# A two-layer mLSTM and attention trunk on one core: a later start for the third pair of weight buffers, and two products in the other order

## The chip, the core and the metric

The kernel runs on one core of one Trainium2 chip. Its time is device microseconds from launch to end, the median of several runs. The engines that matter are TensorE (PE, with PEld for its weight loads), VectorE (DVE), ScalarE (ACT) and SyncE (SP), which here only issues the transfers between HBM and the on-chip memory. Each engine works through its own instructions in the order in which they were written for it; an instruction that waits holds up all that stand behind it on that engine.

## The reference

The input `x` is 512 tokens of width 2048 in float32. Layer one is an mLSTM with 8 heads, layer two an attention over chunks of 64 with 16 heads. What the change touches are the projections of the first layer, its output product, and the projections of the second layer:

```python
h = modulate(rmsnorm(x, g_pre[l]), shift, scale)
proj = h @ w_in                                   # q, k, v, o, z, gates of layer one
ht = mlstm_chunkwise(q, k, v, li, lf)             # 8 heads
y = sigmoid(o) * rmsnorm(ht, g_head) * silu(z)
x = x + gate * rmsnorm(y @ w_out, g_post[l])      # 4096 -> 2048
kv = hkv @ kv_w                                   # shared keys and values
qz = h @ w_in_b                                   # queries and gate of layer two
```

## The kernel before

**Products in float32.** A float32 matrix is split in two parts, `hi` and `lo`: ACT rounds it (L180, `wh<-wr`), DVE subtracts (L181, `wl<-wr,wh`). Each product of 128 rows is three passes on PE, all issued at L229: hi by hi, hi by lo, lo by hi.

**The stream of weights.** All weights are read as one list of 586 pieces of up to 128x1024, in the order of use; `wpiece` (L186) handles the next one: it loads it (`wr`, L198), splits it into `wh` and `wl`, and gives these to the products. Pieces 0 to 289 are `a_w_in`, 290 to 401 `a_w_out`, 402 to 481 `kv_w`, 482 to 545 `b_w_in`, the rest `b_w_out`. In the order rows below `wh291` is `wh` of piece 291; the number behind it only tells tiles apart.

**Buffers.** Pool `wp` has two buffers for `wr` and two pairs for `wh` and `wl`. While `spare` is set, pieces whose number is a multiple of 3 take their `wr` from a third buffer in another pool; while `spare_w` is set, they take `wh` and `wl` from a third pair there (L214). `spare_w` is unset for heads 3 to 7 of layer one (L671). Behind the last head (h = 7) the pools of that layer are closed (L774 to L776) and a pool `wx` for the third pair is opened (L777). Pools reuse memory: a tile of a new pool waits for the tiles that had the memory before. `wx` lies where temporaries of the heads lay, among them `dd`, which divides the head's output by its norm. The tiles `y` of heads 4 to 7 lie where the gates `zo` of the last head lay, so that they wait until these are written out (`ysc<-zo`, L768).

**The step from the last head to `a_w_out`.** The last head ends in: products `ps_n`, sums of squares through PE (`ps_q`), then on `dd` a multiply-add (L762), a clamp (L763), a square root on ACT (L764), a reciprocal (L765), four products with the gates (L767) and four writes (L768). Then `rows(0, ...)` multiplies the first group of 512 output columns: 16 pieces, 290 to 305, each with 24 products of 512 columns (four row tiles, two blocks of 128, three passes). Its other operand `y` is read back (`yr`, L795 and L800) and split by ACT and DVE (`y<-yr`), two tiles for each piece. In between run sums for the second layer's scale, `adq` (loads L913, sums L900, in a fixed order): five buffers, so a load waits for the sum five before. The next groups of columns (from piece 306) take two row tiles at a time.

**Seven products for eight.** `proj_s` (L274) multiplies two blocks of weight columns by two halves of the tokens with seven products instead of eight, in PSUM banks D, C, A and B. It uses sums of weight blocks, made on DVE (`ws`, L205 to L207) and split into `wsh` and `wsl`, beside the piece itself (`wh`, `wl`); two buffers each. One product is three passes for each of two blocks, with 256 columns. Heads 3 to 7, the keys and the attention's projections go through it.

Which instruction comes where on an engine is set by the scheduler of the programming layer when the program is built: by the order of the code, priorities (weights go ahead of other work) and the buffers that it finds free.

Of the kernel before, what the change touches and what calls it, by code (L numbers as in the profile page):

```python
# [49 lines left out]
def pair_pieces(f, merged=False):  # L50


    sk, nk = list(range(f)), list(range(f, KT // 2))
    n = len(nk)
    assert n <= f
    out = [([[a]], [b]) for a, b in zip(sk, nk)]
    return out + [([sk[i : i + 2]] if merged else [[k] for k in sk[i : i + 2]], []) for i in range(n, f, 2)]
# [75 lines left out]
def hybrid_trunk(ctx, tc, xT, xN, c, adaT, cols, wst, wg, ext, kc, out):  # L133
# [9 lines left out]
    def pool(name, bufs=1, **kw):  # L143
        return tc.tile_pool(name=name, bufs=bufs, reuse_waits="tile", **kw)
# [39 lines left out]
    spare, spare_w = [None], [None]  # L184
# [46 lines left out]
    def mm3(ps, ah, al, bh, bl, start, stop):  # L231
        mm(ps, ah, bh, start, False)
        mm(ps, ah, bl, False, False)
        mm(ps, al, bh, False, stop)
# [15 lines left out]
    def proj_b(mat, xs, pss, ms=range(4), kts=KT, at={}, late=0, summed=0, pl=None):  # L250

        held = []
        for k0 in range(0, kts, 2):
            if k0 in at:
                at[k0]()
            held.append((k0, wpiece(mat, pl=pl, diff=k0 < 2 * summed)))
            if k0 >= kts - 2 * late and k0 < kts - 2:
                continue  # L260
            for group in [[pm] for pm in zip(pss, ms)] if k0 in (0, kts - 2) else [list(zip(pss, ms))]:
                for ka, parts in held:
                    for j in range(2):
                        k = ka + j
                        x = xs(k) if callable(xs) else xs[k]
                        for ps, m in group:
                            t = slice(m * P, (m + 1) * P)
                            other = j == 1 and m > 1 and len(parts) > 1
                            w = slice(0, 512) if other else slice(j * 512, (j + 1) * 512)
                            hi, lo = parts[other]  # L270
                            mm3(ps, x[:, 0, t], x[:, 1, t], hi[:, w], lo[:, w], k == 0, k == kts - 1)
            held.clear()

    def proj_s(mat, xs, ss, f, z1, z2, name, pl, bufs, at={}, merged=False, other=False):  # L274

        D, C, A, B = [(newa if other and n != "d" else newp)(f"ps_{n}{name}") for n in "dcab"]
        pieces = pair_pieces(f, merged)
        begun = set()  # L280
        h0, h1_ = slice(0, 256), slice(256, 512)
        for i, (sk, nk) in enumerate(pieces):
            if i in at:
                at[i]()
            main, *extra = wpiece(mat, [len(ks) for ks in sk], pl, bufs)

            def acc(ps, cols, parts, b, x, last):
                start = id(ps) not in begun
                begun.add(id(ps))
                w = slice(b * P, (b + 1) * P)  # L290
                mm3(ps[:, cols], parts[0][:, w], parts[1][:, w], x[:, 0, :], x[:, 1, :], start, last)

            def eight():
                b0 = 4 * sum(len(ks) for ks in sk)
                for m, k in enumerate(nk):
                    for j in range(2):
                        for t, ps in enumerate((A, B)):
                            acc(ps, slice(0, S), main, b0 + 4 * m + 2 * j + t, xs[2 * k + j], False)

            def seven(g, ks):  # L300
                ns = len(ks)
                b0 = 4 * sum(len(u) for u in sk[:g])
                end = i == len(pieces) - 1 and g == len(sk) - 1
                for ps, cols, t, at_, x, last in (
                    (D, h1_, 0, 1, lambda k: ss[k][1], False),
                    (D, h0, 0, 0, lambda k: xs[2 * k][:, :, h0], end),
                    (C, h0, 1, 1, lambda k: ss[k][2], False),
                    (C, h1_, 1, 0, lambda k: ss[k][0], end),
                    (A, h1_, 1, 2, lambda k: xs[2 * k + 1][:, :, h1_], False),
                    (A, h0, 0, 3, lambda k: xs[2 * k + 1][:, :, h0], end),  # L310
                    (B, h0, 0, 2, lambda k: ss[k][3], end),
                ):
                    if i == 0 and g == 0 and ps is B:
                        eight()
                    for j, k in enumerate(ks):
                        acc(ps, cols, extra[g] if t else main, (0 if t else b0) + at_ * ns + j, x(k), last and j == ns - 1)

            if i:
                eight()
            for g, ks in enumerate(sk):  # L320
                seven(g, ks)
        with tc.high_priority(AHEAD):
            nc.scalar.copy(z1[:, 0, :], D[:, h0])
            nc.vector.tensor_tensor(z2[:, 1, :], z1[:, 0, :], D[:, h1_], op=ALU.add)
            nc.vector.tensor_tensor(z1[:, 1, :], z2[:, 1, :], C[:, h0], op=ALU.add)
            nc.vector.tensor_tensor(z2[:, 0, :], z2[:, 1, :], C[:, h1_], op=ALU.add)
            nc.vector.tensor_tensor(z2[:, 1, :], z1[:, 1, :], C[:, h1_], op=ALU.add)
            nc.vector.tensor_tensor(z1, z1, A.rearrange("p (a t) -> p a t", a=2), op=ALU.add)
            if f < KT // 2:
                nc.vector.tensor_tensor(z2, z2, B.rearrange("p (a t) -> p a t", a=2), op=ALU.add)  # L330
            else:
                nc.vector.tensor_tensor(z2[:, 0, :], z2[:, 0, :], B[:, h0], op=ALU.add)
# [30 lines left out]
    def newp(name):  # L363
        return psP.tile([P, S], F32, tag="p", name=name)
# [409 lines left out]
    hqst.close()  # L774
    hst.close()
    phA.close()  # L776
    spare_w[0] = ctx.enter_context(pool("wx", side="right"))  # L777


    kst = ExitStack()  # L780
# [29 lines left out]
    def gate_row(layer, g, gb=ssum):  # L810

        nc.sync.dma_start(gb, ggd[layer, 4 * g : 4 * g + 4, :].rearrange("k p -> (k p)").partition_broadcast(P))

    def evac(ps, m, g, dst, gated=True, later=None):
        if later is not None:
            later[m] = lambda: nc.vector.tensor_tensor(dst, ps, gb, op=ALU.mult)
        elif gated:
            nc.vector.tensor_tensor(dst, ps, gb, op=ALU.mult)
        else:
            nc.vector.tensor_copy(dst, ps)  # L820
        nc.scalar.activation(newa(f"sqy{m}_{g}"), ps, AF.Square, accum_out=ssq[:, 4 * m + g : 4 * m + g + 1])
# [64 lines left out]
    def rows(g, ms, xs, at={}):  # L886
        ps = [newp(f"ps_y0_{g}_{m}") for m in ms]
        proj_b("a_w_out", xs, ps, ms=ms, kts=32, at=at)
        with tc.high_priority(AHEAD):
            for p, m in zip(ps, ms):  # L890
                yt[m].append(rp.tile([P, S], F32, tag="r", name=f"y{m}_{g}"))
                evac(p, m, g, yt[m][g])
# [4 lines left out]
    def scale_sums():  # L897

        for i, j, a in scale_in:
            pin(nc.vector.tensor_tensor_reduce(  # L900
                a, a, scQ[j], 1.0, mod[:, i : i + 1] if j else col(CB + i), ALU.mult, ALU.add, mod[:, i : i + 1]
            ))
        scale_in.clear()
# [13 lines left out]
    def scale_steps(*ks):  # L917
        at = {k: lambda: (scale_sums(), scale_load()) for k in ks}
        return at | {k + 2: scale_load for k in ks}

    gate_row(0, 0)
    rows(0, range(4), y_tile, scale_steps(4, 10, 16, 22, 28))
    for pair, ms in enumerate(PAIRS):
        for g in range(1, 4):
            at = scale_steps(4, 12, 20, *([28] if g < 3 else [])) if pair == 0 else {}
            if pair == 0 and g == 3:
                at[28] = lambda: (scale_sums(), amul_cols(2, 48 + KT, GPRE + KT))
            if pair == 1 and g == 1:
                at = {2: lambda: residual(0), 4: lambda: residual(1)}
                at |= {20 + 4 * i: lambda i=i: turned(0, [i], False) for i in range(3)}  # L930
            if pair == 1 and g == 2:
                at = {2: lambda: turned(0, [3], False)}
            if pair == 1 and g == 3:
                at = {k: lambda k=k: [key_input(i, kept(i, slice(0, 2 * P)), slice(0, 2 * P)) for i in range(k // 2 - 1, k // 2 + 1)] for k in range(2, 32, 4)}
            gate_row(0, g)
            rows(g, ms, ys, at)
# [352 lines left out]
```

## Time and profile before

| | before |
|---|---|
| median of 3 runs | 2808.89 us (2805.28 to 2811.35) |
| the profiled execution's own time | 2808.36 us |
| its span, first to last instruction | 2806.6 us |
| granted TensorE clock, mean | 0.995 |
| PE, DVE, ACT busy | 98%, 79%, 50% of the span |
| chain that ended last, by engine | PE 88%, DVE 5%, DMA 4%, ACT 2% |
| moved by DMA | 527.12 MB, mean 188 GB/s |

PE is the engine that sets the time. The span is 1.8 us less than the execution's own time: what lies before the first and behind the last instruction. Two kinds of rows carry the argument: windows, which give for a stretch of time the busy time of each engine and the granted clock, and timelines, which list an engine's instructions with the idle time before each and what ended it.

### The profile page before, as it was taken

How to read it: one execution, taken by the hardware profiler on the slowest of the kernel's cores; microseconds unless marked ns; L12 is line 12 of the kernel's file. 1: busy time of each engine (PE TensorE's matmuls, PEld its weight loads, DVE VectorE, ACT ScalarE, POOL GpSimd, SP SyncE). 2: the span in 40 equal slices, each digit the busy share in tenths (PEclk: the TensorE clock that was granted, in tenths of full speed). 3: DMA queues.
4: the chain of work that ended last, by engine and by line, in shares of the span. 5: the costliest groups of instructions: out<-in, count | busy, mean ns of one | idle time of the engine just before them, and what ended most of it. 6: DMA issues, size and time to landing. Idle time of an engine off the chain costs nothing.

```text
span 2806.6 us, 42903 instructions
## 1 busy us (share of the span) xinstructions
PE 2761.2 (98%) x16400; PEld 2455.8 (88%) x16400; DVE 2220.3 (79%) x3664; ACT 1408.2 (50%) x2023; POOL 0.2 (0%) x4
## 2 busy tenths in 40 slices
PE   7999999999999999999997999999999999999998
PEld 5887888888999999989997888888998899999887
DVE  7986979768997887978877467567986798898676
ACT  4234524334555555555556234568534566666523
POOL 0000000000000000000000000000000000000000
PEclk9999999999999999999998999999999999999999
DMA  8975787865332333323337599788535544444686
GB/s 297 311 248 178 231 317 254 290 220 171 100 113 91 99 115 102 114 91 106 113 98 236 173 295 300 253 265 289 176 131 179 168 128 122 129 121 124 218 309 238
DMA packets 185016, 527.12 MB, mean 188 GB/s; under 512 B 19893, under 2 KB 38357, under 8 KB 184169
## 3 DMA queue, kind: packets, MB, share of 16 engines
q1 hardware_dynamic: 184810, 524.38, 56.6%
q8 instruction: 128, 2.10, 0.3%
q14 instruction: 78, 0.64, 0.1%
HBM read 490.69 MB, written 38.85 MB: 189 GB/s over the span
## 4 chain that ended last, share of the span: by engine, by line
PE 88%; DVE 5%; DMA 4%; ACT 2%; issue 1%; SPq 0%; DVEq 0%; ACTq 0%
PE ps_y L229 16%; PE ps_v L229 12%; PE ps_azo L229 4%; PE ps_o L229 4%; PE ps_kv L229 4%; PE ps_czo L229 4%; PE ps_dzo L229 4%; PE ps_qk L229 3%; PE ps_z L229 3%; PE ps_l L229 3%; PE ps_az L229 3%; PE ps_cz L229 3%; PE ps_dz L229 3%; PE ps_bzo L229 2%; PE ps_s L229 2%; PE ps_lead L229 2%
## 5 line engine op out<-in xcount | busy, mean ns | idle before, releaser
L180 ACT CAST wh<-wr 128x1024 fp32r<-128x1024 f32 (+3 forms) x586 | 585.7, 1001 | 751.2 <-PE ps_y L229 220.4
L181 DVE TENSOR_TENSOR wl<-wr,wh 128x1024 fp32r<-128x1024 f32 (+3 forms) x586 | 678.4, 1159 | 257.7 <-ACT wh L180 255.6
L229 PE MATMUL ps_y<-wh,y 128*128 128x512 f32 x1536 | 478.5, 392 | 9.2 <-ACT wh L180 9.2
L229 PEld LDWEIGHTS ps_y<-wh,y 128*128 128x128 f32 x1536 | 289.3, 189 | 69.5 <-ACT wh L180 9.6
L180 ACT CAST wsh<-ws 128x768 fp32r<-128x768 f32 (+2 forms) x240 | 188.8, 787 | 309.5 <-DVE ws L207 102.0
L229 PE MATMUL ps_y<-wl,y 128*128 128x512 f32 x768 | 300.2, 391 | 5.1 <-DVE wl L181 5.1
L229 PE MATMUL ps_v<-wh,h 128*128 128x512 f32 x896 | 285.5, 390 | 0.0
L181 DVE TENSOR_TENSOR wsl<-ws,wsh 128x768 fp32r<-128x768 f32 (+2 forms) x240 | 215.1, 898 | 87.0 <-ACT wsh L180 85.2
L229 PEld LDWEIGHTS ps_v<-wh,h 128*128 128x128 f32 x896 | 168.2, 188 | 34.5
L229 PEld LDWEIGHTS ps_y<-wl,y 128*128 128x128 f32 x768 | 144.9, 189 | 35.5 <-DVE wl L181 5.8
L229 PE MATMUL ps_v<-wl,h 128*128 128x512 f32 x448 | 174.7, 390 | 0.0
L205 DVE TENSOR_TENSOR ws<-wr 128x512 f32<-128x512 f32 (+1 forms) x208 | 139.4, 671 | 31.4 <-DMA wr<-in_wst 29.9
L229 PE MATMUL ps_kv<-wh,hkv 128*128 128x512 f32 x512 | 159.6, 390 | 0.0
L396 DVE CUSTOM_DVE_ANT_0 ada<-ada,scB,mod 128x1024 f32<-128x1024 f32 x96 | 123.0, 1282 | 17.3 <-DMA ada<-in_adaT 16.0
L396 DVE CUSTOM_DVE_ANT_0 ada<-ada,scB,cl 128x1024 f32<-128x1024 f32 x96 | 122.8, 1281 | 16.6 <-DMA ada<-in_adaT 16.5
L229 PEld LDWEIGHTS ps_kv<-wh,hkv 128*128 128x128 f32 x512 | 96.1, 188 | 20.3 <-ACT wh L180 0.4
L229 PE MATMUL ps_kv<-wl,hkv 128*128 128x512 f32 x256 | 100.0, 391 | 1.2 <-DVE wl L181 1.2
L229 PE MATMUL ps_l<-h,wh 128*128 128x512 f32 x320 | 99.2, 392 | 0.6 <-ACT q L489 0.4
L229 PEld LDWEIGHTS ps_v<-wl,h 128*128 128x128 f32 x448 | 84.2, 188 | 17.2 <-issue 0.9
L207 DVE TENSOR_TENSOR ws<-wr 128x256 f32<-128x256 f32 (+1 forms) x208 | 85.7, 413 | 2.7
L206 DVE TENSOR_TENSOR wr<-ws,wr 128x256 f32<-128x256 f32 (+1 forms) x208 | 85.5, 411 | 1.8
L229 PE MATMUL ps_qk<-h,wh 128*128 128x512 f32 x256 | 79.4, 390 | 0.0
(402 smaller groups left out, 6502.9 us busy)
## 6 DMA issues: line engine op xcount, KB each, us to landing
wr<-in_wst SPq DMA_DIRECT2D x520, 512.0 KB, 4.0
ada<-in_adaT SPq DMA_DIRECT2D x224, 512.0 KB, 6.0
adq<-in_adaT SPq DMA_DIRECT2D x64, 256.0 KB, 5.8
xt<-nsc SPq DMA_DIRECT2D x48, 256.0 KB, 4.2
wr<-in_wst SPq DMA_DIRECT2D x30, 256.0 KB, 4.5
yr<-ysc SPq DMA_DIRECT2D x28, 256.0 KB, 6.2
wr<-in_wst SPq DMA_DIRECT2D x16, 384.0 KB, 6.0
bsc<-in_ext SPq DMA_DIRECT2D x16, 320.0 KB, 6.1
```

Of the source, the lines that this page charges most:

```text
L180: nc.scalar.copy(hi, src)
L181: nc.vector.tensor_tensor(lo, src, hi.bitcast(F32), op=ALU.subtract)
L205: nc.vector.tensor_tensor(t[:, : 2 * w], r[:, w : 3 * w], r[:, : 2 * w], op=ALU.subtract)
L206: nc.vector.tensor_tensor(r[:, w : 2 * w], t[:, w : 2 * w], r[:, :w], op=ALU.add)
L207: nc.vector.tensor_tensor(t[:, 2 * w :], r[:, 3 * w :], r[:, w : 2 * w], op=ALU.subtract)
L229: nc.tensor.matmul(ps, a, b, start=start, stop=stop)
L396: pin(nc.vector.tensor_tensor_reduce(at, at, (sc or scB)[:, j * D // 2 : (j + 1) * D // 2], 1.0, mod[:, i : i + 1] if j else col(CB + i), ...
```

## The change

Two edits. `spare_w` is set to `wx` not where the pool is opened but behind the first group of output columns: pieces 290 to 305 all take the two pairs of `wp`, and piece 306 is the first in the third pair. The pool's place in memory stays. And in `proj_s` the last two products into bank A change places: the one with `wh` (block 3, tokens 0 to 255) comes first, the one with `wsh` (block 2, tokens 256 to 511) second.

```diff
-                    (A, h1_, 1, 2, lambda k: xs[2 * k + 1][:, :, h1_], False),
-                    (A, h0, 0, 3, lambda k: xs[2 * k + 1][:, :, h0], end),
+                    (A, h0, 0, 3, lambda k: xs[2 * k + 1][:, :, h0], False),
+                    (A, h1_, 1, 2, lambda k: xs[2 * k + 1][:, :, h1_], end),
                     (B, h0, 0, 2, lambda k: ss[k][3], end),
...
-    spare_w[0] = ctx.enter_context(pool("wx", side="right"))
+    wx = ctx.enter_context(pool("wx", side="right"))
...
     rows(0, range(4), y_tile, scale_steps(4, 10, 16, 22, 28))
+    spare_w[0] = wx
     for pair, ms in enumerate(PAIRS):
```

On ACT, in the last head, while its products `ps_n` are evacuated (`sqs`, `sq`):

```order
 L755 ACTIVATE sqs7_14172<-ps_n7_0_14173 128x512
 L755 ACTIVATE sq7_1_14197<-ps_n7_1_14186 128x512
-L180 CAST wh292_14355<-wr292_14353 128x1024
+L180 CAST wh291_14311<-wr291_14309 128x1024
 L755 ACTIVATE sq7_2_14212<-ps_n7_2_14201 128x512
```

Before, piece 292 was cast here, ahead of 291; now it is 291.

On DVE, where the last head's `dd` is finished (L762 to L765) and applied to the gates (L767):

```order
+L181 TENSOR_TENSOR wl293_14400<-wr293_14397,wh293_14399 128x1024
 L762 SCALAR_TENSOR_TENSOR dd7_14168<-ps_q7_14231,dd7_14168 128x512
-L756 SCALAR_TENSOR_TENSOR zo7_3_0_13922<-ps_n7_3_14216,cl_99,zo7_3_0_13922 128x512
 L763 TENSOR_SCALAR dd7_14168<-dd7_14168 128x512
 L765 RECIPROCAL dd7_14168<-dd7_14168 128x512
+L181 TENSOR_TENSOR wl294_14440<-wr294_14437,wh294_14439 128x1024
 L767 TENSOR_TENSOR zo7_0_0_13202<-zo7_0_0_13202,dd7_14168 128x512
 L767 TENSOR_TENSOR zo7_1_0_13442<-zo7_1_0_13442,dd7_14168 128x512
 L767 TENSOR_TENSOR zo7_2_0_13682<-zo7_2_0_13682,dd7_14168 128x512
 L767 TENSOR_TENSOR zo7_3_0_13922<-zo7_3_0_13922,dd7_14168 128x512
-L181 TENSOR_TENSOR wl291_14312<-wr291_14309,wh291_14311 128x1024
+L181 TENSOR_TENSOR wl295_14488<-wr295_14485,wh295_14487 128x1024
```

The difference of 291 stood behind all of it; now those of 293 and 294 stand in it, and 295 behind.

On DVE further on, among the `adq` sums (each an `ISA` row on its tile and one that reads out the sum):

```order
 L900 ISA adq73_0_14615,mod_102<-adq73_0_14615,scQ0_14347,cl_99 128x512
 L900 ISA mod_102 128x1
+L181 TENSOR_TENSOR wl300_14704<-wr300_14701,wh300_14703 128x1024
 L900 ISA adq74_0_14657,mod_102<-adq74_0_14657,scQ0_14347,cl_99 128x512
 L900 ISA mod_102 128x1
-L181 TENSOR_TENSOR wl297_14572<-wr297_14569,wh297_14571 128x1024
```

At this point of the sums DVE made piece 297 before and makes piece 300 now. Five sums stand ahead of each of 299, 300 and 301 in the changed order, as they stood ahead of 296, 297 and 298.

## The prediction

> **What bounds the kernel now.** I read the page's busy shares first, to see whether any engine is full.
>
> ```profile
> span 2806.6 us, 42903 instructions
> PE 2761.2 (98%) x16400; PEld 2455.8 (88%) x16400; DVE 2220.3 (79%) x3664; ACT 1408.2 (50%) x2023; POOL 0.2 (0%) x4
> ```
>
> TensorE is busy for all but 45.4 us of the span. An edit that changes no product can win only what lies in those 45.4 us, or what makes a product slower than it could be. So the next view is the busy time by stage.
>
> ```profile
> 835.00:1497.00 662.00, 660.41 (x4709) 625.72 (x4708) 547.88 (x850) 366.79 (x468) 0.00 (x0) 1.00 0.32 104
> 1497.00:1550.00 53.00, 38.63 (x168) 31.37 (x168) 43.61 (x67) 31.34 (x49) 0.00 (x0) 0.84 0.87 289
> 1550.00:1608.00 58.00, 58.00 (x257) 48.03 (x256) 21.39 (x33) 11.86 (x12) 0.00 (x0) 1.00 0.49 163
> 2245.00:2630.00 385.00, 382.94 (x3006) 371.96 (x3005) 340.42 (x746) 255.20 (x437) 0.00 (x0) 1.00 0.44 134
> ```
>
> Columns: stretch, its length, busy time of PE, PEld, DVE, ACT, POOL, granted clock, DMA share, GB/s. The long stages (heads 4 to 7, attention) lose 1.6 and 2.1 us. The 53 us around 1520 lose 14.4 us, and there the clock is 0.84. This is the step from the first layer's last head to its output product. The list of waits, cut to that place, names what PE waits for:
>
> ```profile
> PE ps_y L229 <- ACT wh L180: 9.2, 1, 9.2
> PE ps_y L229 <- DVE wl L181: 5.1, 1, 5.1
> ```
>
> Two waits, once each. The timelines of PE, ACT and DVE (start, length, what ran, idle before it) say which weights those are.
>
> ```profile
> 1504.45 0.48 PE L229 MATMUL ps_y<-wh,y 128*128 128x512 f32 x1
> ...
> 1509.99 0.91 PE L229 MATMUL ps_q<-sp_q,ones_r 128*128 128x512 f32 x2
> 1520.14 1.22 PE L229 MATMUL ps_y<-wh,y 128*128 128x512 f32 x2 [9.25 <-ACT wh L180]
> 1526.46 0.79 PE L229 MATMUL ps_y<-wl,y 128*128 128x512 f32 x1 [5.09 <-DVE wl L181]
> ```
> ```profile
> 1501.96 1.05 ACT L180 CAST wh<-wr 128x1024 fp32r<-128x1024 f32 x1
> ...
> 1511.09 1.04 ACT L180 CAST wh<-wr 128x1024 fp32r<-128x1024 f32 x1
> ...
> 1518.53 0.63 ACT L764 ACTIVATE dd<-dd 128x512 f32<-128x512 f32 x1 [1.78 <-DVE dd L763]
> 1519.07 1.03 ACT L180 CAST wh<-wr 128x1024 fp32r<-128x1024 f32 x1
> ```
> ```profile
> 1504.83 1.22 DVE L181 TENSOR_TENSOR wl<-wr,wh 128x1024 fp32r<-128x1024 f32 x1
> ...
> 1519.19 3.35 DVE L765 RECIPROCAL dd<-dd 128x512 f32<-128x512 f32 x1 [0.69 <-ACT dd L764]
> 1522.58 2.50 DVE L767 TENSOR_TENSOR zo<-zo,dd 128x512 f32<-128x512 f32 x4
> 1525.18 1.23 DVE L181 TENSOR_TENSOR wl<-wr,wh 128x1024 fp32r<-128x1024 f32 x1
> ```
>
> By the order of before, the casts at 1501.96 and 1511.09 are pieces 292 and 293, and the one at 1519.07 is 291, which PE needs first. 291 is a multiple of 3, so it takes the third pair, whose memory held tiles of the head that is just ending: its cast stands behind the square root of `dd` (L764), its difference behind the reciprocal and the last products (L765, L767). PE uses 290 at 1504.45 and then has nothing until both are through.
>
> **What the change removes.** PE is idle from 1510.90 (1509.99 + 0.91) to 1526.46, except for two products, which at full pace take 0.45: 15.1 us. What follows is slow as well:
>
> ```profile
> 1526.46 241.51 PE ps_y L229 x1054
> ...
> 1790.60 84.36 PE ps_y L229 x372
> ```
>
> In the chain of work a product takes 84.36/372 = 0.2268 us later on, but the 1054 from 1526.46 take 241.51 instead of 239.0: 2.5 us more. The granted clock (second last but one column) explains it:
>
> ```profile
> 1515.00:1520.00 5.00, 0.00 (x0) 0.00 (x0) 4.30 (x8) 3.20 (x4) 0.00 (x0) 0.50 0.82 234
> ...
> 1535.00:1540.00 5.00, 5.00 (x23) 4.13 (x22) 5.00 (x9) 5.00 (x10) 0.00 (x0) 1.00 0.88 280
> ```
>
> The clock is halved in the idle time and full again by 1535. So 15.1 + 2.5 = **17.6 us** go if PE never waits here. The Trainium skill (TensorE: Matmul & The Clock Gate, Part 1: The HAM clock gate) puts both the idle time that halves the clock and the busy time that restores it at about 3.4 us. By that page each restart costs an estimated 1.7 us, two of them 3.4, and 18.5 would go in place of 17.6; the trace shows half clock but the smaller loss, and I keep the row.
>
> Does PE really not wait? In the changed order 291 stands where 292 stood on ACT and DVE (cast 1501.96, difference done by 1506.05), in the buffers of 289, long left by PE. Its load is one of the pair issued here:
>
> ```profile
> 1495.84 1.17 SPq L198 DMA_DIRECT2D wr<-in_wst  x2
> ...
> 1523.37 2.35 SPq L768 DMA_DIRECT2D ysc<-zo  x4
> ```
>
> It needs to be ready when 290 ends, at 1504.45 + 24 x 0.2268 = 1509.9: four us to spare. A piece lasts 5.44 us; with the 0.45 of `ps_q`, now inside 292, PE reaches 293 at 1521.2, 294 at 1526.7, 299 at 1553.9, 300 at 1559.3 and 301 at 1564.7. 292 and 293 stand in the places of 293 and behind the last early `y` split, done by 1513.9 and 1518.8. 294 is behind the reciprocal: `ps_q` runs some nine products into 292, at 1517.4; behind the difference of 293 (1518.8) come two short steps on `dd` and the square root, together about 1.7, and the reciprocal, 3.35, to about 1523.9, and the difference of 294 (1.22) ends at 1525.1, with 1.8 us to spare.
>
> **What it adds.** Sixteen pieces run on two pairs. A cast can start only when PE leaves the piece two before, 5.44 us ahead of need; cast and difference take 2.3 of it. The rest is cover for whatever DVE's order puts ahead of the difference. Two things stand there. First the `y` splits of heads 4 to 7, which wait for the last `ysc` write:
>
> ```profile
> 1531.89 5.31 ACT L180 CAST y<-yr 128x512 fp32r<-128x512 f32 x10 [11.80 <-DMA ysc<-zo]
> ...
> 1532.55 6.11 DVE L181 TENSOR_TENSOR y<-yr,y 128x512 fp32r<-128x512 f32 x10 [6.14 <-ACT y L180]
> ```
>
> Before, they began 6.2 us after the last write's issue (1523.37 + 2.35). Now this write stands on SP behind the load of 298, which waits for the difference of 295 (1529.0), so it leaves at 1529.5 and the splits begin at 1533.5 to 1535.7. Sixteen splits of 0.61, the differences of 297 and 298, and five `adq` sums of 0.82 bring the difference of 299 to an end at 1552 to 1553.9; needed 1554.1. Second, the `adq` sums, five of them ahead of each of 299, 300 and 301:
>
> ```profile
> 1548.68 1.22 DVE L181 TENSOR_TENSOR wl<-wr,wh 128x1024 fp32r<-128x1024 f32 x1
> 1550.27 0.75 DVE L900 CUSTOM_DVE_ANT_0 adq<-adq,scQ,cl 128x512 f32<-128x512 f32 x1 [0.37 <-DMA adq<-in_adaT]
> 1550.95 0.08 DVE L900 DVE_READ_ACCUMULATOR2_ANT mod<- 128x1 f32 x1
> ...
> 1554.61 1.22 DVE L181 TENSOR_TENSOR wl<-wr,wh 128x1024 fp32r<-128x1024 f32 x1
> ...
> ...
> 1560.66 1.22 DVE L181 TENSOR_TENSOR wl<-wr,wh 128x1024 fp32r<-128x1024 f32 x1
> ```
> ```profile
> 1545.91 3.21 SPq L913 DMA_DIRECT2D adq<-in_adaT  x5
> ```
> ```profile
> adq<-in_adaT SPq DMA_DIRECT2D x64, 256.0 KB, 5.8
> ```
>
> Before, such a round took 5.9 to 6.0 us, because the sums wait for their loads; PE takes 5.44. The third pair hid that. Now 300 ends at 1558 to 1560 (needed 1559.5). 301 adds the load of `adq78`, queued on SP behind the load of 303, which waits for 300: 0.5 + 4.4 to land + 0.82 + 1.22, so 1565 to 1567 against 1564.9. The 4.4 is what the first of the five above took, issued at 1545.91 behind a weight load and summed on landing at 1550.27; the page's median for such loads is 5.8, but this one follows a pause of SP. I take **1.0 us** of new waiting; ends: 0, and 3.5 with every landing at 5.8. Behind 301 only one sum stands before 302, and from 306 the third pair is in use, as before.
>
> The swap of two products moves the last reader of `wsh` by six products, 0.72 us later, in every seven-product piece. It adds no instruction. Cost between a gain of 1.6 (all idle time of heads 4 to 7) and the price in the third rival; nearest is the row of that stage, which hardly waits, so 0.
>
> **Sum.** The profiled execution took 2808.36 us, 0.5 under the median of the runs: 2808.4 - 17.6 + 1.0 = **2791.8**.
>
> **Rivals.**
> 1. The wait comes back on two buffers: landings above 5.8 us in a stage at 0.87 of DMA put 299 to 301, or 294 behind the reciprocal, several us late: 3.5 to 10 us back, 2795 to 2802. For it: the DVE rounds are longer than PE's piece. Against: only three rounds. The same page of the Trainium skill would add a halved clock to any single wait above about 3.4 us; the 9.25 above shows it, no wait that I expect is so long.
> 2. The wait doesn't go: something else holds PE at 1510 as long, or a load lands 10 us later: 2803 to 2814. Against: the order puts 291 in front.
> 3. Slower: the later release of `wsh` reaches PE.
>
> ```profile
> ACT wsh L180 <- PE ps_az L229: 92.8, 46, 2.7
> ...
> L205 DVE TENSOR_TENSOR ws<-wr 128x512 f32<-128x512 f32 (+1 forms) x208 | 139.4, 671 | 31.4 <-DMA wr<-in_wst 29.9
> ```
> ```profile
> 884.29 1.44 PE ps_czo L229 x12
> ```
> ```profile
> 1483.97 1.22 DVE L181 TENSOR_TENSOR wl<-wr,wh 128x1024 fp32r<-128x1024 f32 x1
> ...
> 1486.76 0.40 PE L229 MATMUL ps_dzo<-h1s,wh 128*128 128x256 f32 x2
> ```
>
> ACT does wait for these releases, 46 times in the attention alone, and 208 pieces have them; the six products are half of the 1.44 us of twelve. If PE paid 0.72 each time it were 150 us; from 0.08 us a piece (16.6/208) the gain is gone, and 0.12 gives 2817. Against: the difference of 288 ends at 1485.2 and PE, which began 288 at 1486.76, had 1.6 us in hand, twice the shift.
>
> **How the numbers follow.** Forecast (2788 to 2795) 0.71; rival 1 0.14; rival 2 0.06; rival 3 0.05; better still, with the idle time of other stages gone too, 0.04. A measurement of this kernel tells about 0.2% (5.6 us) from no change; faster by more than that: 0.71 + 0.14 + 0.04 = 0.89, within 0.06, slower 0.05. The range 2787.5 to 2798 holds the forecast and half of rival 1, about 0.8; its ends also take in the spread of the runs, 3 us either way.
>
> **What would show it.** Right: no PE wait above 1 us between 1500 and 1550, a granted clock of 1.00 there, the casts in the order 290, 291, 292; PE some 17 us ahead by 1555, with one or two waits under 2 us on `wl` near 1560 to 1567. Wrong: a PE wait above 3 us at 1510 to 1570, or PE idle in heads 4 to 7 or the attention above the 1.6 and 2.1 us of before.

## The result, and the profile after

The changed kernel takes 2788.69 us in the median of four runs (2784.57 to 2793.66), beside 2810.12 for the kernel before in the same comparison: ratio 0.9928, interval 0.9907 to 0.9948. The execution that was profiled took 2784.57, where before took 2808.36: 23.8 us less. The prediction was 2791.8, 16.6 less. The page's head, and the four stages whose rows were shown of before (the attention's begins 17 us earlier; the other three have the same bounds as before):

```profile
span 2782.7 us, 42823 instructions
...
PE 2751.1 (99%) x16400; PEld 2452.1 (88%) x16400; DVE 2217.3 (80%) x3664; ACT 1401.9 (50%) x2025; POOL 0.2 (0%) x4
```
```profile
835.00:1497.00 662.00, 661.31 (x4718) 626.67 (x4717) 548.79 (x853) 369.58 (x473) 0.00 (x0) 1.00 0.32 104
1497.00:1550.00 53.00, 53.00 (x247) 44.41 (x246) 42.70 (x60) 34.58 (x52) 0.00 (x0) 1.00 0.89 295
1550.00:1608.00 58.00, 56.47 (x250) 46.33 (x249) 33.65 (x62) 16.67 (x22) 0.00 (x0) 1.00 0.70 225
2228.00:2613.00 385.00, 384.34 (x3032) 376.32 (x3031) 342.81 (x753) 252.65 (x443) 0.00 (x0) 1.00 0.45 140
```

The 53 us around 1520, where PE was busy for 38.63 at a clock of 0.84, are full now, at 1.00. A new hole of 1.5 us stands in the next window. PE's busy time in total fell by 10.1 us though the products are the same 16400: part of what went was never idle time.

To see where, I take the time between the first products of two pieces of the weight list, from the timelines of PE. The columns are the stages in the order of the list.

| pieces | work | before, us | after, us | difference |
|---|---|---|---|---|
| 0–149 | before and in heads 0 to 3 | 693.89 | 695.43 | +1.54 |
| 150–289 | the end of head 3, and heads 4 to 7 | 780.68 | 778.91 | -1.77 |
| 290–299 | first output columns | 72.95 | 55.11 | **-17.84** |
| 300–305 | the same, end | 32.64 | 34.51 | **+1.87** |
| 306–401 | other output columns | 264.76 | 264.76 | 0.00 |
| 402–481 | keys and values | 342.87 | 341.39 | -1.48 |
| 482–545 | attention | 396.09 | 390.33 | **-5.76** |
| 546–584 | last product | 178.92 | 178.70 | -0.22 |

Where the text below gives a time for heads 4 to 7, it is that of pieces 150 to 289. Three terms are bold; the other rows together are -1.9, and the experiments show how far such rows move by themselves. The first term is the one that the change was predicted to remove. On ACT and DVE the cast and the difference of 291 now come here (start, length, what ran, idle before):

```profile
1502.70 1.05 ACT L180 CAST wh<-wr 128x1024 fp32r<-128x1024 f32 x1 [1.05 <-DMA wr<-in_wst]
...
1511.24 1.05 ACT L180 CAST wh<-wr 128x1024 fp32r<-128x1024 f32 x1
...
1515.29 1.05 ACT L180 CAST wh<-wr 128x1024 fp32r<-128x1024 f32 x1
```
```profile
1505.55 1.22 DVE L181 TENSOR_TENSOR wl<-wr,wh 128x1024 fp32r<-128x1024 f32 x1
...
1520.73 3.35 DVE L765 RECIPROCAL dd<-dd 128x512 f32<-128x512 f32 x1 [0.70 <-ACT dd L764]
1524.00 1.16 DVE L181 TENSOR_TENSOR wl<-wr,wh 128x1024 fp32r<-128x1024 f32 x1
```

By the order, the casts are 291, 292 and 293; 291 is whole at 1506.8, 2.7 us ahead of PE, which finishes 290 at 1509.5. The difference of 294 is the one behind the reciprocal, done at 1525.2.

The second term is the new wait. The list of waits of PE on weights in this stage has one row (total, times, longest); PE, DVE and SP show it:

```profile
PE ps_y L229 <- DVE wl L181: 1.5, 1, 1.5
```
```profile
1566.57 0.50 PE L229 MATMUL ps_y<-wl,y 128*128 128x512 f32 x1 [1.53 <-DVE wl L181]
```
```profile
1564.62 0.75 DVE L900 CUSTOM_DVE_ANT_0 adq<-adq,scQ,cl 128x512 f32<-128x512 f32 x1 [2.04 <-DMA adq<-in_adaT]
...
1565.30 1.22 DVE L181 TENSOR_TENSOR wl<-wr,wh 128x1024 fp32r<-128x1024 f32 x1
```
```profile
1559.28 0.33 SPq L198 DMA_DIRECT2D wr<-in_wst  x1
1559.66 1.25 SPq L913 DMA_DIRECT2D adq<-in_adaT  x2
```

Piece 301's difference stands behind a sum whose load leaves SP at 1559.66, behind the weights of 303, and lands at 1564.6.

The third term was not predicted. These are windows cut exactly at the attention's first and last piece, of before and of after:

```profile
2217.67:2613.76 396.09, 394.91 (x3157) 386.92 (x3156) 351.01 (x752) 257.70 (x431) 0.00 (x0) 1.00 0.43 131
```
```profile
2199.83:2590.16 390.33, 390.33 (x3157) 386.46 (x3156) 348.77 (x752) 251.28 (x431) 0.00 (x0) 1.00 0.43 133
```

The same 3157 products, the same clock; PE is idle for 1.2 us before and not at all after. The other 4.6 us are in "busy" time. In the rows below a product of 256 columns is listed with 0.28 us, whether the next one starts 0.12 or 0.28 us behind it: a hold shorter than that leaves no gap on PE, and shows only in the weight loads. These are the waits of PEld in that window of before (after has none), then the last block of a head's transposes in before, as the weight load and with the products around it, and such a block in after:

```profile
PEld ps_t L1092 <- DVE pt L181: 2.3, 12, 0.2
PEld ps_t L1092 <- DVE s L1083: 2.0, 4, 0.8
```
```profile
2417.59 0.14 PEld L1092 LDWEIGHTS ps_t<-kcs,s 128*128 128x128 f32 x1 [0.20 <-DVE pt L181]
```
```profile
2416.87 0.38 PE L1092 MATMUL ps_t<-kcs,s 128*128 128x128 f32 x2
2417.00 0.48 PE L229 MATMUL ps_dz<-h2s,wh 128*128 128x256 f32 x2
2417.32 0.28 PE L229 MATMUL ps_dz<-h2s,wl 128*128 128x256 f32 x1
2417.60 0.33 PE L1092 MATMUL ps_t<-kcs,s 128*128 128x128 f32 x1
```
```profile
2421.39 0.38 PE L1093 MATMUL ps_t<-kcs,s 128*128 128x128 f32 x2
2421.53 0.48 PE L229 MATMUL ps_dz<-h2s,wh 128*128 128x256 f32 x2
...
2422.56 0.28 PE L229 MATMUL ps_dz<-h,wl 128*128 128x256 f32 x1
2422.68 0.28 PE L1093 MATMUL ps_t<-kcs,s 128*128 128x128 f32 x1
```

In the attention each head's scores `s` are transposed block by block on PE (`ps_t`), and ACT and DVE split the result (`pt`). Before, the last block stands three products behind the block ahead of it, and DVE has not yet read the bank that it takes: the product in front takes 0.28 from start to start where it takes 0.12 otherwise. After, it stands nine products behind and waits for nothing. Over the 71 places where a product is followed by a transpose, the mean start to start is 177 ns before and 120 after. Added up over the stage, the steps to a transpose took 4.0 us less after, those between transposes 1.1 and those behind them 0.8; all other steps from one start to the next add up to the same within 0.1 us. So the whole gain lies at the transposes, and the other products are as fast in either order.

### The profile page after: what moved, and what is told of

It reads as the page before. It is cut to its first block, busy times and chain, and to the rows that moved or that the text cites. A ratio compares the mean times of both kernels' runs of the same rounds, so it can differ in the third digit from the quotient of the medians.

```text
span 2782.7 us, 42823 instructions
## 1 busy us (share of the span) xinstructions
PE 2751.1 (99%) x16400; PEld 2452.1 (88%) x16400; DVE 2217.3 (80%) x3664; ACT 1401.9 (50%) x2025; POOL 0.2 (0%) x4
## 4 chain that ended last, share of the span: by engine, by line
PE 84%; DVE 6%; DMA 5%; issue 2%; ACT 2%; SPq 0%; DVEq 0%; ACTq 0%
PE ps_y L229 14%; PE ps_v L229 12%; PE ps_kv L229 5%; PE ps_o L229 4%; PE ps_azo L229 4%; PE ps_czo L229 4%; PE ps_dzo L229 4%; PE ps_az L229 3%; PE ps_cz L229 3%; PE ps_dz L229 3%; PE ps_qk L229 3%; PE ps_z L229 3%; DMA ada<-in_adaT 2%; PE ps_bzo L229 2%; PE ps_s L229 2%; PE ps_n L229 2%
```

## Experiments

Each kernel ran beside the kernel before on the same chip, five rounds. Diffs are against the changed kernel.

**The changed kernel again.**

> The changed kernel again, beside the others. Theory: as before minus 21 us; waits at 301 alone, 1.5 us. A rival that takes the attention's gain for chance of one execution: its heads would then last 25.1 us or more here.

2789.85 us (2785.78 to 2790.6), ratio 0.9928 [0.9915, 0.994]. Attention 390.32 and pieces 290 to 299 in 55.00, as in the first profile. But pieces 300 to 305 took 36.37, 3.7 more than before, though the wait was hardly longer:

```profile
PE ps_y L229 <- DVE wl L181: 1.8, 1, 1.8
```
```profile
1565.00:1570.00 5.00, 3.17 (x11) 2.54 (x11) 3.59 (x6) 0.86 (x1) 0.00 (x0) 0.83 0.78 267
1570.00:1575.00 5.00, 5.00 (x20) 4.07 (x19) 0.00 (x0) 1.01 (x1) 0.00 (x0) 0.82 0.51 167
```

The clock (third column from the end) falls behind this wait: the row from 1570 to 1575 has 20 products, where that of the first profile has 24 at a clock of 1.00. That is the other half of the 3.7 us.

**One edit at a time.** First, the third pair late, the two products in the old order:

```diff
-                    (A, h0, 0, 3, lambda k: xs[2 * k + 1][:, :, h0], False),
-                    (A, h1_, 1, 2, lambda k: xs[2 * k + 1][:, :, h1_], end),
+                    (A, h1_, 1, 2, lambda k: xs[2 * k + 1][:, :, h1_], False),
+                    (A, h0, 0, 3, lambda k: xs[2 * k + 1][:, :, h0], end),
```

> Third pair from piece 306 on, bank A in the order of before. Theory: the wait at the step to the output product goes in full (17.9 us from piece 290 to 300), one wait of 1.5 to 2 us at piece 301 comes, and the attention stays as it was before (each head 25.1 to 25.4 us), since its order on PE is that of before: about 16 us below before. Rival: the 5.8 us that the changed kernel gained in the attention come from the earlier arrival of that stage, not from the order of bank A; then this run gains them as well, about 22 us.

2795.59 us (2794.11 to 2798.71), ratio 0.9953 [0.994, 0.9967]: 13.3 less than before. Pieces 290 to 299 in 55.00, 300 to 305 in 35.75 (two waits, 2.5 us together), attention 395.75.

Second, the new order of the two products, the third pair early:

```diff
-    wx = ctx.enter_context(pool("wx", side="right"))
+    spare_w[0] = ctx.enter_context(pool("wx", side="right"))
...
-    spare_w[0] = wx
```

> Bank A in the new order alone, third pair from piece 290 as before. Theory: both waits at piece 291 stay (9.2 and 5.1 us, clock 0.50 behind them), and the attention gains 0.28 us a head, 5 to 6 us in all, because its order on PE is that of the changed kernel: 4 to 6 us below before. Rival: the new order is worth nothing, and the time is that of before within 1 us; second rival: the later release of the sums costs PE something in heads 4 to 7, and the time is above before.

2804.71 us (2802.45 to 2809.04), ratio 0.9983 [0.9974, 0.9992]: 4.2 less. Its list of waits has the old pair of rows unchanged, and its attention takes 390.35:

```profile
PE ps_y L229 <- ACT wh L180: 9.2, 1, 9.2
...
PE ps_y L229 <- DVE wl L181: 5.1, 1, 5.1
```

So each edit has its own place: the late third pair removes the wait at 291 and nothing in the attention, the swap the reverse. 13.3 and 4.2 make 17.5, where both together gave 19.1 on this chip.

**The third pair early, but not for the two pieces that meet the head's tail.** The new order of the products, and:

```diff
-            pw = spare_w[0] if spare_w[0] and i % 3 == 0 else wp
+            pw = spare_w[0] if spare_w[0] and i % 3 == 0 and i not in (291, 294) else wp
...
+    spare_w[0] = ctx.enter_context(pool("wx", side="right"))
...
-    spare_w[0] = wx
```

> Bank A in the new order, third pair from piece 290 on but not for 291 and 294, so that it begins with 297. Theory: no wait at 291, since nothing of the last head is waited for; the third pair also takes the five sums one piece further ahead, so that the wait of 1.5 us at 301 goes: 1.5 to 2 us below the changed kernel, PE without a wait from 1497 to 1608. Rival: the wait at 301 is one of DMA for the weights themselves, and stays.

2787.22 us (2785.25 to 2791.06), ratio 0.9922 [0.9909, 0.9935]. No wait of `ps_y` at all: 55.01 for 290 to 299 and 32.64 for 300 to 305. With the third pair in use from 297 the wait at 301 is gone, so that wait is a price of two pairs. Its whole time isn't told apart from that of the changed kernel; heads 4 to 7 took 782.10 in its profile, 3.2 more than in the changed kernel, with the same order on VectorE and ScalarE up to there.

**The third pair early, but not for 291 alone** (as above with `i not in (291,)`), so that 294 is the first in it.

> New order of the two products; the third pair opened where it was before, but piece 291 alone takes the two common pairs. 294 takes the third, and its cast and difference now stand behind those of 296. Theory 1 (the old wait was the place of the third pair's cast and difference behind the tail of the head, for whichever piece first takes it): PE waits for wh and wl of 294 at about 1526, 2.1 and 1.4 us by the order and the durations of before, so pieces 290 to 300 take 57.5 to 59 in place of 55.1, no wait at 301 (300 to 306: 32.64). Theory 2 (it was 291's place alone): no wait at 294, 290 to 300 in 55.0, whole time as with 291 and 294 both left out, about 2787. If the clock falls after such short waits, 1 to 2 us more.

2788.64 us (2784.16 to 2793.77), ratio 0.993 [0.9918, 0.9942]. Pieces 290 to 299 took 57.97, and PE waits at 294:

```profile
1530.61 1.21 PE L229 MATMUL ps_y<-wh,y 128*128 128x512 f32 x4 [2.12 <-ACT wh L180]
...
1532.06 0.50 PE L229 MATMUL ps_y<-wl,y 128*128 128x512 f32 x1 [0.24 <-DVE wl L181]
```

Theory 1 holds: the wait goes with the third pair, to whichever piece is first in it; 2.1 on the cast as expected, 0.24 where 1.4 was expected on the difference. Here the clock stayed at 1.00.

**The sums moved out of the first group** (two steps of them there in place of five; the rest later):

```diff
-    rows(0, range(4), y_tile, scale_steps(4, 10, 16, 22, 28))
+    rows(0, range(4), y_tile, scale_steps(22, 28))
...
-            at = scale_steps(4, 12, 20, *([28] if g < 3 else [])) if pair == 0 else {}
+            at = scale_steps(4, 10, 16, 22, *([28] if g < 3 else [])) if pair == 0 else {}
```

> The changed kernel, with the 64 sums of the scale moved: two steps of them in place of five in the first group of output columns, more in the later groups. The same work in another order. Theory 1 (the wait of 1.5 to 1.8 us at piece 301 is the rounds of sums ahead of the differences of 299 to 301): no wait there, pieces 300 to 306 in 32.64 in place of 34.5 to 36.4, whole time about 2787.5. Theory 2 (the wait comes from the two pairs alone, or from the load of the weights): the wait stays, 34.5 or more.

2786.82 us (2783.06 to 2792.34), ratio 0.9926 [0.9914, 0.9938]. Pieces 300 to 305 in 32.64, no wait on weights there, 306 to 401 in 264.76 as ever. The wait at 301 needs both: two pairs, and the rounds of sums ahead of the differences.

**The swap in the attention alone, and everywhere but there** (third pair late in both). In the first the old order is kept for all but the attention's `z`; the second reverses the condition:

```diff
+                if name[0] == "z" and name[1].isdigit():
+                    (p5, c5, t5, a5, x5, _), (p6, c6, t6, a6, x6, _) = seq[4:6]
+                    seq[4:6] = [(p6, c6, t6, a6, x6, False), (p5, c5, t5, a5, x5, end)]
```

> Third pair late as in the changed kernel; the two products of bank A in the new order in the attention's projections alone (head, key and z products elsewhere in the old order). Theory 1 (the swap works in the attention alone, because there a product of the old order stands in front of a transpose and holds PE): attention, pieces 482 to 546, 390.3 us as in the changed kernel, whole time about 2790. Theory 2 (the swap works through the heads, and the 5.7 us seen in the attention were that execution's): attention about 396, whole time about 2795 as with the old order everywhere.

> Third pair late; the new order of the two products everywhere but in the attention's projections. Theory 1 (the swap works in the attention alone): attention 395.8 to 396.1 us, whole time about 2795. Theory 2 (it works through the heads): attention 390.3 whatever its own order, or the loss of time elsewhere; whole time about 2790.

In the attention alone: 2785.85 us (2784.58 to 2788.53), ratio 0.9917 [0.9904, 0.993], attention 390.37. Everywhere else: 2792.02 (2788.42 to 2800.5), ratio 0.9944 [0.9931, 0.9957], attention 395.41. Theory 1 holds. Elsewhere the order of the two products shows nothing: heads 4 to 7 took 780.6 us with the old and 779.6 with the new, the keys and values 341.1 and 341.2. The first of the two also had a wait of 2.4 us at 301, and behind it the clock fell:

```profile
1570.00:1575.00 5.00, 5.00 (x17) 3.96 (x16) 0.87 (x1) 0.00 (x0) 0.00 (x0) 0.66 0.89 284
```

**Is it the transposes' place?** The swap does three things in the attention: two products change places; most transposes move 6 to 8 products back; and some work on DVE and ACT is re-ordered. The next kernels keep the old order of the products (as in the first single edit) and move the transposes by their priority:

```diff
+                with tc.high_priority(-40):
+                    nc.tensor.transpose(ps[:, P * (i - j) : P * (i - j + 1)], pr[i][:, P * j : P * (j + 1)], ident)
```

> Third pair late, the two products of bank A in the old order everywhere; in the attention the transposes of the scores have a lower priority, so that most of them stand 9 to 12 products later on PE and those of the last two blocks 36 to 40 later (the changed kernel has most of them 6 to 8 later). The same products in the same order among themselves. Theory 1 (the order of the products itself costs nothing; what the changed kernel gains in the attention is that the transposes come after their scores and banks are ready): attention 390.3 to 391 us, no product ahead of a transpose above 130 ns in the mean, whole time about 2790. Theory 2 (the old order of the products costs the time, by where the sums of weight blocks come): attention 395.5 as with the old order, whole time about 2795.

2793.35 us (2790.99 to 2800.31), ratio 0.9948 [0.9936, 0.9961]; attention 397.40, more than either order. A miss, for a reason that its waits in the attention show:

```profile
PEld ps_o L229 <- DVE pt L181: 3.6, 8, 1.0
PEld ps_t L1094 <- DVE s L1084: 1.2, 2, 0.8
```

The products that read the transposes (`ps_o`) now wait for them, which they never did before. And the hold ahead of the transposes is not gone: 173 ns from start to start in the mean, over 58 places, and the wait for `s` is much as with the old order's own places (1.5 there). Later isn't better by itself. The same priority in the changed kernel, together with the moved sums:

> The changed kernel with the sums of the scale moved out of the first group and the transposes of the attention at lower priority. Theory 1: no wait at piece 301 (300 to 306: 32.64) and attention 389 to 390.3, since the 1 us that PE still waits at the last transpose of a head goes; whole time 2785 to 2788. Theory 2: the late transposes hold up the products that read them, attention above 390.3.

2792.77 us (2787.84 to 2797.89), ratio 0.9943 [0.993, 0.9955]; attention 393.41, 3.1 more than with the changed kernel's places. Pieces 300 to 305 took 32.64, so the sums' part held; the transposes' part didn't, and the time expected was missed.

Last, priorities for each block, chosen so that every transpose stands within one product of its place in the changed kernel (those behind the last head's products excepted), with the old order of the products:

```diff
+                with tc.high_priority(-{(0, 1): 36, (1, 1): 36, (0, 2): 40, (0, 3): 39, (1, 2): 40, (1, 3): 39, (3, 3): 11}.get((j, i), 0)):
+                    nc.tensor.transpose(ps[:, P * (i - j) : P * (i - j + 1)], pr[i][:, P * j : P * (j + 1)], ident)
```

> Third pair late, the two products of bank A in the old order everywhere; in the attention the transposes stand, to within one product, at the places that the changed kernel has (6 to 8 products later than the old order puts them; only behind the last head's products they differ). VectorE and ScalarE keep nearly the order of the old products. Theory 1 (it is the transposes' place on PE): attention 390.3 to 391 us, products ahead of a transpose 120 ns in the mean, whole time about 2790. Theory 2 (it is the order of the other work on VectorE and ScalarE, which makes scores and banks late): the products ahead of a transpose stay near 170 ns, attention 394 to 396, whole time about 2795. Between the two: both have a share.

2791.91 us (2789.03 to 2794.67), ratio 0.9933 [0.992, 0.9947]. Its attention and the waits of PEld in it:

```profile
2201.04:2592.92 391.88, 391.49 (x3158) 386.71 (x3156) 352.84 (x752) 257.88 (x431) 0.00 (x0) 1.00 0.44 132
```
```profile
PEld ps_t L1094 <- DVE pt L181: 1.0, 3, 0.5
```

Of the 5.4 us between 395.75 and 390.33, moving the transposes brings 3.9, with the products in the old order. The attention lies between the ranges of the two theories, and so does the time ahead of a transpose: 146 ns in the mean, over 85 places (14 more, since a single product now stands between two transposes once in each of 14 heads). Both have a share. DVE's order is nearer to the old one than to the changed kernel's, but ACT's differs from both, so the 3.9 are the transposes' places together with what moves around them.

The row of waits for `s` is gone, that for the banks is smaller (2.5 in 13 waits in the run with the old places). Its three waits stand before the last block of three heads, at 2300, 2350 and 2450, nine products behind the block ahead, as in the changed kernel: the place is the same there, but DVE has not yet read the bank. So about 1.0 of the remaining 1.5 comes from when DVE does its work, and not from the place; the rest wasn't told apart.

## Why the prediction was right, and where it was not

**The removed wait: right.** 17.6 was predicted for the idle time and the half clock, 17.84 measured between the first products of 290 and 300, 17.95 in the run with this edit alone. The cause is shown from both sides: with the third pair back at 291 the 9.2 and 5.1 come back; with 291 alone taken out of it, 294 pays. Piece 300 was put at 1559.3 and came at 1559.17; the difference of 294 was put at 1525.1 and ended at 1525.2. The clock was 1.00 throughout.

**The new wait: the place right, the size too small.** It came at 301, on `wl`, behind the one sum and the one load that were named. That load took 4.96 from issue to the sum, where 4.4 was taken, so the wait was 1.5 and not 1.0; the stage lost 1.87. Seven profiles have this wait, and there the stage lost 1.5 to 4.7. The bounds, 0 and 3.5, held it in the first profile, but not in the repeat (3.7) nor in the run with the swap in the attention alone (4.7). What they left out is the clock. The first rival said that no wait that was expected was long enough to halve it; 1.8 and 2.4 us were followed by a lower clock.

**The swap: the step that failed.** "It adds no instruction. Cost between a gain of 1.6 (all idle time of heads 4 to 7) and the price in the third rival; nearest is the row of that stage, which hardly waits, so 0." It gained 5.76 in the attention, outside these bounds. Two things were wrong in it. It followed only the reader of `wsh` and its buffer, and not what else stands between the products: with another order of the code the scheduler also puts the transposes elsewhere. And it took the idle time of PE as all that a stage can gain, from the heads and not even from the attention, though the prediction had begun with a second place to look, products that are slower than they could be. The attention's idle time was 1.2 us, and 4.6 were in products that PE held back while it counted as busy.

**The sum.** -17.6 + 1.0 + 0 was predicted. -17.84 + 1.87 - 5.76 was measured, and -1.9 in stages for which nothing was claimed. In the medians the miss is small, 2791.8 against 2788.69, and that is partly luck: the drop was 21.4 where 16.6 was forecast, and a gain that the forecast put at nothing made up for a wait that cost more than was forecast. The run with the late third pair alone, which has only the forecast's two terms, took 2795.59.

**The rivals.** The wait did not come back on two buffers beyond the 1.87 us in the first profile, though the transfers took a share of 0.89 ahead of it; with the fall of the clock, 3.7 and 4.7 in two later profiles reach the lower end of what that rival gave back (3.5). The later release of `wsh` didn't reach PE: heads 4 to 7 lost 0.7 us of PE's time after, 1.6 before. What happened is nearest to the case "better still, with the idle time of other stages gone too".

## What to carry to other kernels

When a pool takes over memory of a phase that is ending, its first tile inherits that phase's tail: give it to work that is needed late, and look which work has it. Compare the busy time of the same instructions in two kernels: stalls inside "busy" show there and in the waits of the weight loads, not in the idle time. And of a changed order of code, read the new order on every engine and for all that stands between the moved instructions; a gain can lie there, and so can a loss: the transposes' places were worth 3.9 us in one run and cost 1.6 in another.

## What the runs showed that was not expected

- **The clock fell after short waits, and not after each.** Between 100 and 2770 us the thirteen profiles have 22 single waits of PE of 1.2 to 2.9 us. Behind five of them, of 1.8, 2.3, 2.4, 2.8 and 2.9 us, the clock was halved for 3.41 us, which costs 1.7; behind the other seventeen, of 1.2 to 2.3 us, it stayed at 1.00. The changed kernel again, in the stretch at half clock:

```profile
1568.35:1571.76 3.41, 3.41 (x10) 2.67 (x9) 0.24 (x1) 0.00 (x0) 0.00 (x0) 0.50 0.88 289
```

  The Trainium skill (TensorE: Matmul & The Clock Gate, Part 1: The HAM clock gate) gives an idle window of about 3.4 us that runs free of the kernel. A free-running window fits that like waits end differently; its length doesn't fit 1.8 us, and the measurement decides.
- **A stage can move with nothing changed in it.** Heads 4 to 7 took 778.9 to 784.2 us in these profiles, with the same order on VectorE and ScalarE in the changed kernel (778.91) and in that with only the swap (784.21); the first products of two heads waited 0.7 us for `wl` in the one, 3.8 in the other, and behind the longest of these waits, 2.8 us, the clock fell (0.91 from 1010 to 1015, 0.75 from 1015 to 1020), some 1.7 us more. Together that is 4.8 of the 5.3 us between the two. Those 5.3 us are nearly as large as the attention's whole gain, so that gain is read from its stage, not from the sum.
